# RWKV-7 chain in a hybrid trunk: outputs of four chunks issued together, five state tiles, start tile of the substitution written by memsets

## The chip, the cores and the metric

The kernel runs on one core of one Trainium2 chip. The metric is the device time of one execution in microseconds (us). The engines named below are TensorE (PE in the profile; its weight loads are PEld), VectorE (DVE), ScalarE (ACT), GpSimd (POOL) and SyncE (SP), which here only issues DMAs.

## The reference

One layer of a decoder trunk over 1024 tokens of 1024 features, float32. After an RMS norm one projection feeds three groups of heads; their outputs (256 + 512 + 256 features) are concatenated, projected and added to the residual; a gated MLP with a short convolution and a last norm follow.

```python
h = rms_norm(x, norm_mix)
p_conv, p_nsa, p_rwkv = split(h @ w_in)
mix = concatenate([conv_mixer(p_conv), nsa_mixer(p_nsa), rwkv7_mixer(p_rwkv)])
x = x + mix @ w_out
x = x + conv_ffn(rms_norm(x, norm_ffn), w_gate, conv_w, conv_b, w_up, w_down)
return rms_norm(x, norm_final)
```

The change lies in `rwkv7_mixer`: four heads of 64, each with a 64 x 64 state S that is updated token by token, followed by a norm over each head (group norm), a bonus term and a gate:

```python
def step(S, (r, w, k, v, kk, a)):
    sa = einsum('bhvk,bhk->bhv', S, -kk)
    S = S * w + outer(sa, kk * a) + outer(v, k)
    return S, einsum('bhvk,bhk->bhv', S, r)
```

## The kernel before

The 1024 tokens stay in chunks of 64 for RWKV. Two heads form a pair (j = 0, 1), the tokens form two halves of eight chunks (h = 0, 1), so there are four units, 00, 01, 10 and 11. Each unit passes through three steps. S (`rwkv_prep`, `rwkv_mats`, L487) builds the chunks' matrices; at its end a strictly triangular 32 x 32 system per chunk and head is solved by substitution in 31 pairs of operations on GpSimd (L532, L534), which starts from an identity: L527 copies the constant tile sI (128 x 256) into sT. The rows of the system come back into sN by a DMA from the scratch tensor dn, and sT goes out to dt by DMAs at L537. V (`rwkv_solve`, L542) finishes the inverse for 64 tokens. C (`rwkv_chain`, L583) walks the eight chunks in order.

A chunk in C is a serial loop through two engines: PE multiplies the state H with AT (L595), DVE adds the result into VA (L596), PE forms the state's increment from VA and KB (L601), DVE writes the next state into rH (L608, the two diagonal blocks). Beside this loop the chunk's output is summed in PSUM: r times the old state (L612) plus GR times VA (L615), into its slice of the bank py. There are two rH tiles, used in turn. py is taken from the PSUM tag "rw", which has two banks, before the first chunk; the products of L595 and L601 take turns in what is left of this tag. After the eighth chunk DVE and ACT do the group norm on py (L621 to L632), PE transposes the result (L635) and multiplies the gate (L640), and z (gz) goes to the DRAM tensor md by L642.

The order of the program is the list "lora r0 S00 conv taps V00 S01 keys q C00 V01 r1a cmp0 r1b cmp1 r1c S10 C01 V10 S11 C10 V11 C11", then the attention tiles (`attn_tile`), then the output projection. A tile scheduler simulates the kernel at build time and settles each engine's own order from it; S, V and C are emitted at high priority, so their instructions are put between those of projections (C00) and attention (the other chains).

In an attention tile PE computes scores (L897, L898), transposes the probabilities (L922) and multiplies V (L930); ACT empties the result into a mix tile (L936), and SP stores it to md (L937). The compressed branch has L843, L866, L869. The output projection works by tiles of 128 tokens, the last tile (7) first: two loads of md (`mix`, L988, four 128-feature slabs each: the first holds convolution and RWKV, the second attention), a split of each into two parts (ACT L120, DVE L121), 48 matmuls at L229, and the residual xn (L992). w_out's last pieces (wraw, L971), the norm's gains (grow, L1340) and the first MLP weights (wr and wraw, L1060) are loaded by SP around that place. A wait on any of SP's DMAs holds back what SP has behind it.

Of the kernel before, what the change touches and what calls it, by code (L numbers as in the profile page):

```python
# [7 lines left out]
F32 = mybir.dt.float32  # L8
# [8 lines left out]
P = 128  # L17


class K:  # L20
# [293 lines left out]
    def rwkv_params(self):  # L314
        nc, a = self.nc, self.a
        self.lw_w = self.mc.tile([P, 256], F32, name="lw_w")
        nc.sync.dma_start(self.lw_w[0:32, :], a["rwkv_w2"][0])
        nc.sync.dma_start(self.lw_w[32:64, :], a["rwkv_a2"][0])
        nc.sync.dma_start(self.lw_w[64:128, :], a["rwkv_g2"][0])

        self.bones = self.mc.tile([P, P], F32, name="bones")
        nc.gpsimd.memset(self.bones, 0.0)
        nc.gpsimd.memset(self.bones[0:64, 0:64], 1.0)
        nc.gpsimd.memset(self.bones[64:128, 64:128], 1.0)

        self.rH = [self.mc.tile([P, P], F32, name=f"rH{i}") for i in range(2)]
        for t in self.rH:
            nc.gpsimd.memset(t, 0.0)

        self.sN = self.mc.tile([P, 1024], F32, name="sN")  # L330
        self.sT, self.sI, self.sTT = (self.mc.tile([P, 32, 8], F32, name=n) for n in ("sT", "sI", "sTT"))
        self.sx = self.mc.tile([P, 80], F32, name="sx")
        self.DF = self.mc.tile([P, 16, 32], F32, name="DF")
        nc.gpsimd.memset(self.sI, 0.0)
        for g in range(4):
            r = self.sI[g * 32:g * 32 + 32].rearrange("p a b -> p (a b)")
            nc.gpsimd.memset(r[:, g * 8:256:33], 1.0)

        self.rst = self.mc.tile([P, 512], F32, name="rst")
        nc.gpsimd.memset(self.rst, 1.0)  # L340
        nc.gpsimd.memset(self.rst.rearrange("p (c t) -> p c t", t=64)[:, :, 0:1], 0.0)

        self.gmask = self.mc.tile([P, P], F32, name="gmask")
        nc.gpsimd.memset(self.gmask, 1.0)
        for base in (0, 64):
            for col, strict in ((0, 1), (64, 0)):
                blk = self.gmask[base:base + 64, col:col + 64]
                nc.gpsimd.affine_select(out=blk, in_=blk, pattern=[[1, 64]], compare_op=ALU.is_ge, fill=0.0,
                                        base=-strict, channel_multiplier=-1)
# [135 lines left out]
    def rwkv_mats(self, u):  # L485
        nc = self.nc
        v, s, pe = nc.vector, nc.scalar, nc.tensor  # L487
        dn = self.dram.tile([32, 32, 32], F32, name=f"dn{u.j}{u.h}")
        u.dt = self.dram.tile([16, 32, 4, 8], F32, name=f"dt{u.j}{u.h}")
        u.dtt = self.dram.tile([32, 8, 4, 32], F32, name=f"dtt{u.j}{u.h}")  # L490

        u.GA, u.GR = ([self.rb([P, 8, 64], name=n) for _ in range(2)] for n in ("GA", "GR"))
        for q in range(2):
            pts = [self.bank(u.tp) for _ in range(2)]
            for c in range(4):
                for hp in range(2):
                    r = slice(hp * 64, hp * 64 + 64)
                    pe.matmul(pts[hp][:, c * P:c * P + P], u.BK[q][r, c].rearrange("p a t -> p (a t)"),
                              u.AR[q][r, c].rearrange("p a t -> p (a t)"), start=True, stop=True)
            for x, G in enumerate((u.GA, u.GR)):  # L500
                for hp in range(2):
                    v.tensor_tensor(G[hp][:, q * 4:q * 4 + 4, :], pts[hp].rearrange("p (a b) -> p a b", b=P)[:, :, x * 64:x * 64 + 64],
                                    self.gmask[:, x * 64:x * 64 + 64].unsqueeze(1).to_broadcast([P, 4, 64]), op=ALU.mult)
        for hp in range(2):
            for blk in range(2):
                p0 = blk * 16 + hp * 8
                nc.sync.dma_start(dn[p0:p0 + 8].rearrange("p s t -> s p t"), u.GA[hp][64 + blk * 32:96 + blk * 32, :, blk * 32:blk * 32 + 32])
        N = self.sN.rearrange("p (a b) -> p a b", b=32)
        for g in range(4):
            nc.sync.dma_start(N[g * 32:g * 32 + 32], dn)  # L510
        u.VA, u.KB = [], []
        for q in range(2):
            VA = self.rb([P, 4, P], name="VA")
            KB = self.rb([P, 4, P], name="KB")
            BK = u.BK[q].rearrange("p c a t -> p c (a t)")
            v.tensor_tensor(BK, BK, u.PC[:, q * 4:q * 4 + 4].unsqueeze(2).to_broadcast([P, 4, P]), op=ALU.mult)
            for dst in (VA, KB):
                pt = self.bank(u.tp)
                for c in range(4):
                    x = u.VAc[q][:, c].rearrange("p a t -> p (a t)") if dst is VA else BK[:, c, :]  # L520
                    pe.transpose(pt[:, c * P:c * P + P], x, self.idn)
                s.activation(dst.rearrange("p c x -> p (c x)"), pt, AF.Copy)
            u.VA.append(VA)
            u.KB.append(KB)

        Tm = self.sT
        nc.gpsimd.tensor_copy(Tm, self.sI)  # L527
        for q in range(31):
            n, w = 31 - q, q // 4 + 1
            x = self.sx[:, 0:n * w].rearrange("p (a b) -> p a b", b=w)  # L530
            v_ = getattr(nc, self.B["sub"])
            v_.tensor_tensor(x, N[:, q, q + 1:32].unsqueeze(2).to_broadcast([P, n, w]),  # L532
                            Tm[:, q, 0:w].unsqueeze(1).to_broadcast([P, n, w]), op=ALU.mult)
            v_.tensor_tensor(Tm[:, q + 1:32, 0:w], Tm[:, q + 1:32, 0:w], x, op=ALU.add)  # L534
        sTT = self.sTT.rearrange("p a b -> p (a b)").rearrange("p (a b) -> p a b", b=32)
        v.tensor_copy(sTT, Tm.rearrange("p a b -> p b a"))
        for g in range(4):  # L537
            nc.sync.dma_start(u.dt[:, :, g, :], Tm[g * 32:g * 32 + 16])
            nc.sync.dma_start(u.dtt[:, :, g, :], sTT[g * 32:g * 32 + 32])
# [43 lines left out]
    def rwkv_chain(self, u):  # L583
        nc = self.nc
        v, s, pe = nc.vector, nc.scalar, nc.tensor
# [1 line left out]
        if u.h == 0:  # L587
            self.H = None
        H = self.H
        py = self.bank("rw")  # L590
        for c in range(8):
            VA, KB = u.VA[c // 4][:, c % 4, :], u.KB[c // 4][:, c % 4, :]
            if H is not None:
                pt = self.bank("rw")
                pe.matmul(pt[64:128, 0:P], u.AT[:, c, :], H, start=True, stop=True)  # L595
                v.tensor_tensor(VA[64:128], pt[64:128, 0:P], VA[64:128], op=ALU.add)  # L596
            last = u.h == 1 and c == 7
            if not last:
                pt = self.bank("rw")
                for x in (slice(0, 64), slice(64, 128)):  # L600
                    pe.matmul(pt[x, 0:P], KB[:, x], VA, start=True, stop=True)  # L601
                Hn = self.rH[c % 2]
                for hp in range(2):
                    x = slice(hp * 64, hp * 64 + 64)
                    if H is None:
                        v.tensor_copy(Hn[x, x], pt[x, x])
                    else:
                        v.scalar_tensor_tensor(Hn[x, x], H[x, x], u.PC[x, c:c + 1], pt[x, x], op0=ALU.mult, op1=ALU.add)  # L608
            ro = slice((c % 2) * 64, (c % 2) * 64 + 64)
            yo = (c // 2) * P  # L610
            if H is not None:
                pe.matmul(py[ro, yo:yo + P], u.r[:, c, :], H, start=True, stop=False)  # L612
            for hp in range(2):
                x = slice(hp * 64, hp * 64 + 64)
                pe.matmul(py[ro, yo + hp * 64:yo + hp * 64 + 64], u.GR[hp][:, c, :], VA[:, x], start=H is None, stop=H is None or hp == 1)  # L615
            H = None if last else Hn
        self.H = H

# [787 lines left out]
```

## Time and profile before

| | |
|---|---|
| three runs | 1479.73, 1487.43, 1487.57 us; median 1487.43 us |
| profiled execution | 1479.4 us, of which the span from first to last instruction is 1477.5 us |
| PE busy | 1388.7 us, 94% |
| DVE, ACT, POOL busy | 68%, 46%, 34% |
| mean granted clock of PE | 0.971 |
| chain of work that ended last | PE 79%, DVE 8%, POOL 4%, DMA 3%, ACT 2% |

The span can be read in four stretches: norms and projections with the convolution up to about 344 us, a change of phase with the attention's loads to 377 us, attention to 704 us with three of the four RWKV chains woven in, output projection and MLP to the end. Busy time counts an engine at work; idle time of PE is what a change can win beside fewer or shorter matmuls, and it is read from the rows where a PE instruction shows an idle time ahead of it.

### The profile page before, as it was taken

To read this page: it belongs to the slowest core of one execution; us is meant where nothing else is said; L and a number is where in the kernel's file an instruction comes from. 1 tells how busy PE (TensorE), PEld (TensorE's weight loads), DVE (VectorE), ACT (ScalarE), POOL (GpSimd) and SP (SyncE) were. 2 spreads that over 40 slices of the span, in tenths; PEclk is the share of its full clock that TensorE was granted. 3 is DMA by queue.
4 is the path that set the end of the run, shared out by engine and by line. 5 is a ranking of instruction groups with operands and counts; after the bars stand their busy time and mean duration, and the time that the engine had idled before them with its cause. 6 is when DMAs were issued, how large, how long until landed. Compare 5 with 4: busy or idle time off the path is not lost.

```text
span 1477.5 us, 22767 instructions
## 1 busy us (share of the span) xinstructions
PE 1388.7 (94%) x7897; PEld 1095.2 (74%) x7897; DVE 1002.7 (68%) x2187; ACT 686.9 (46%) x1377; POOL 499.2 (34%) x607
## 2 busy tenths in 40 slices
PE   6999589998899999999799899999999999999997
PEld 5887457776677676766588677888788788888886
DVE  6347594454868778798257867676775776666685
ACT  5441245624456665678223533343343333445463
POOL 1002996921144066220000144443444442113310
PEclk9999888999899999999899999999999999999999
DMA  6133133436514254542722123332332334986533
GB/s 185 40 107 82 44 103 111 142 84 179 153 33 139 78 154 125 181 150 81 240 89 83 43 93 93 108 107 70 104 113 93 108 100 162 388 280 216 188 92 114
DMA packets 206679, 186.69 MB, mean 126 GB/s; under 512 B 56355, under 2 KB 145764, under 8 KB 206564
## 3 DMA queue, kind: packets, MB, share of 16 engines
q1 hardware_dynamic: 206564, 185.24, 40.3%
q8 instruction: 62, 1.02, 0.3%
q14 instruction: 53, 0.43, 0.1%
HBM read 126.99 MB, written 58.20 MB: 125 GB/s over the span
## 4 chain that ended last, share of the span: by engine, by line
PE 79%; DVE 8%; POOL 4%; DMA 3%; ACT 2%; issue 2%; SPq 1%; ACTq 0%; DVEq 0%; POOLq 0%
PE gb L229 13%; PE mm L229 12%; PE rw L229 10%; PE ga L229 9%; PE gc L229 8%; PE tr L229 5%; PE tr L922 5%; PE av L930 4%; PE mm L897 2%; PE mm L898 2%; POOL sT L534 1%; POOL sx L532 1%; DVE pp L901 1%; POOL cacc L279 1%; DVE pp L915 1%
## 5 line engine op out<-in xcount | busy, mean ns | idle before, releaser
L229 PE MATMUL mm<-hT,whi 128*128 128x512 f32 x608 | 200.3, 409 | 19.6 <-DVE ev L690 14.8
L229 PEld LDWEIGHTS mm<-hT,whi 128*128 128x128 f32 x608 | 115.7, 193 | 48.9 <-ACT whi L120 20.2
L229 PE MATMUL mm<-hT,wlo 128*128 128x512 f32 x304 | 123.0, 407 | 1.9 <-DVE wlo L121 1.9
L925 ACT ACTIVATE pT<-tr 128x512 f32<-128x512 f32 (+1 forms) x152 | 79.9, 536 | 60.6 <-PE tr L922 59.2
L930 PE MATMUL av<-pT,V 128*64 128x128 f32 x1056 | 96.0, 287 | 1.5 <-ACT pT L925 1.5
L1076 POOL TENSOR_TENSOR S<-wraw,wr 128x512 f32<-128x512 f32 x22 | 28.5, 1296 | 192.8 <-DVE or L107 91.1
L922 PE MATMUL tr<-idn,pp 128*128 128x128 f32 x528 | 90.3, 289 | 1.8 <-DVE pp L915 1.8
L279 POOL TENSOR_TENSOR cacc<-cacc,ctap 128x512 f32<-128x512 f32 x60 | 85.1, 1429 | 12.7 <-ACT ctap L278 12.4
L121 DVE TENSOR_TENSOR sp<-rb,sp 128x512 fp32r<-128x512 f32 x66 | 55.6, 842 | 49.4 <-ACT sp L120 49.4
L229 PE MATMUL rw<-woh,mix 128*128 128x512 f32 x240 | 79.5, 407 | 9.0 <-ACT mix L120 9.0
L229 PE MATMUL rw<-sp,sp 128*128 128x512 f32 x330 | 86.0, 389 | 0.0
L229 PE MATMUL tr<-sp,sp 128*128 128x512 f32 x330 | 85.9, 389 | 0.0
L897 PE MATMUL mm<-KH,QS 128*128 128x512 f32 (+2 forms) x192 | 77.7, 411 | 3.1 <-DVE mx L901 2.8
L930 PEld LDWEIGHTS av<-pT,V 128*64 128x64 f32 x1056 | 59.2, 136 | 28.3 <-issue 13.7
L922 PEld LDWEIGHTS tr<-idn,pp 128*128 128x128 f32 x528 | 55.9, 141 | 30.5 <-issue 29.1
L915 DVE TENSOR_SCALAR pp<-pp,sm 128x640 f32<-128x640 f32 (+7 forms) x128 | 76.5, 638 | 0.9
L120 ACT ACTIVATE sp<-rb 128x512 fp32r<-128x512 f32 x66 | 41.6, 630 | 74.1 <-PE tr L229 36.5
L121 DVE TENSOR_TENSOR sp<-b,sp 128x512 fp32r<-128x512 f32 x88 | 72.1, 827 | 5.2 <-ACT sp L120 5.0
L229 PEld LDWEIGHTS mm<-hT,wlo 128*128 128x128 f32 x304 | 58.5, 193 | 18.1 <-DVE wlo L121 3.8
L229 PEld LDWEIGHTS tr<-sp,sp 128*128 128x128 f32 x330 | 61.9, 188 | 12.9
L229 PEld LDWEIGHTS rw<-sp,sp 128*128 128x128 f32 x330 | 61.9, 188 | 12.9
L532 POOL TENSOR_TENSOR sx<-sN,sT 128x60 f32<-128x60 f32 (+24 forms) x124 | 48.0, 387 | 63.0 <-DMA sN<-dn 54.9
(455 smaller groups left out, 3648.8 us busy)
## 6 DMA issues: line engine op xcount, KB each, us to landing
wr<-in_ffn_w_gate_dram SPq DMA_DIRECT2D x44, 256.0 KB
wraw<-in_ffn_w_up_dram SPq DMA_DIRECT2D x44, 256.0 KB
pdS<-prod SPq DMA_DIRECT2D x44, 256.0 KB
b<-pdS SPq DMA_DIRECT2D x44, 256.0 KB
rb<-tdT SPq DMA_DIRECT2D x44, 256.0 KB
pdA<-prod SPq DMA_DIRECT2D x33, 256.0 KB
b<-pdA SPq DMA_DIRECT2D x33, 256.0 KB
wraw<-in_w_in_dram SPq DMA_DIRECT2D x30, 256.0 KB
```

The lines of the kernel that those rows point to most:

```text
L120: self.nc.scalar.activation(hi, src, AF.Copy)
L121: getattr(self.nc, eng).tensor_tensor(lo, src, hi.bitcast(F32), op=ALU.subtract)
L229: mm = lambda l, r, **k: self.nc.tensor.matmul(out, l, r, skip_group_check=more, **k)
L279: nc.gpsimd.tensor_tensor(t[:, o:o + 512], t[:, o:o + 512], z, op=ALU.add)
L532: v_.tensor_tensor(x, N[:, q, q + 1:32].unsqueeze(2).to_broadcast([P, n, w]), Tm[:, q, 0:w].unsqueeze(1).to_broadcast([P, n, w]), op=ALU.mult)
L897: pe.matmul(pts[g][:, 0:n], QS[:, r, g, :], KH[g][hf][:, ks], start=True, stop=False)
L898: pe.matmul(pts[g][:, 0:n], QS[:, r, g, :], KL[g][hf][:, ks], start=False, stop=True)
L915: v.tensor_scalar(Ps[g], Ps[g], sm[:, g:g + 1], None, op0=ALU.mult)
L922: pe.transpose(pt[:, o:o + P], Ps[g][:, kt * P:kt * P + P], self.idn)
L925: s.activation(pT[:, 0:n], pt[:, 0:n], AF.Copy)
L930: pe.matmul(av[g * 64:g * 64 + 64, r * P:r * P + P], self.V[kk // 2][:, kk % 2, vo + g * 64:vo + g * 64 + 64], pT[:, o:o + P], start=first ...
L1076: gp.tensor_tensor(t, x, y, op=op)
```

## The change

The chain no longer multiplies a chunk's output when the chunk is done. It keeps the list Hs of old states, and after chunks 3 and 7 it emits the outputs of four chunks together (new lines L618 and L621); py is taken from the two banks only at the first of these. For that five rH tiles exist, used in a ring that runs on over all units (nH). The constant sI goes; the start tile sT is written by a memset over 128 x 256 and four strided memsets of ones, each time. The matmuls are the same in number and shape.

```diff
--- before.py
+++ after.py
@@ -323,18 +323,15 @@
         nc.gpsimd.memset(self.bones[0:64, 0:64], 1.0)
         nc.gpsimd.memset(self.bones[64:128, 64:128], 1.0)
 
-        self.rH = [self.mc.tile([P, P], F32, name=f"rH{i}") for i in range(2)]
+        self.rH = [self.mc.tile([P, P], F32, name=f"rH{i}") for i in range(5)]
+        self.nH = 0
         for t in self.rH:
             nc.gpsimd.memset(t, 0.0)
 
         self.sN = self.mc.tile([P, 1024], F32, name="sN")
-        self.sT, self.sI, self.sTT = (self.mc.tile([P, 32, 8], F32, name=n) for n in ("sT", "sI", "sTT"))
+        self.sT, self.sTT = (self.mc.tile([P, 32, 8], F32, name=n) for n in ("sT", "sTT"))
         self.sx = self.mc.tile([P, 80], F32, name="sx")
         self.DF = self.mc.tile([P, 16, 32], F32, name="DF")
-        nc.gpsimd.memset(self.sI, 0.0)
-        for g in range(4):
-            r = self.sI[g * 32:g * 32 + 32].rearrange("p a b -> p (a b)")
-            nc.gpsimd.memset(r[:, g * 8:256:33], 1.0)
 
         self.rst = self.mc.tile([P, 512], F32, name="rst")
         nc.gpsimd.memset(self.rst, 1.0)
@@ -524,7 +521,9 @@
             u.KB.append(KB)
 
         Tm = self.sT
-        nc.gpsimd.tensor_copy(Tm, self.sI)
+        nc.gpsimd.memset(Tm, 0.0)
+        for g in range(4):
+            nc.gpsimd.memset(Tm[g * 32:g * 32 + 32].rearrange("p a b -> p (a b)")[:, g * 8:256:33], 1.0)
         for q in range(31):
             n, w = 31 - q, q // 4 + 1
             x = self.sx[:, 0:n * w].rearrange("p (a b) -> p a b", b=w)
@@ -587,9 +586,10 @@
         if u.h == 0:
             self.H = None
         H = self.H
-        py = self.bank("rw")
+        py, Hs = None, []
         for c in range(8):
             VA, KB = u.VA[c // 4][:, c % 4, :], u.KB[c // 4][:, c % 4, :]
+            Hs.append(H)
             if H is not None:
                 pt = self.bank("rw")
                 pe.matmul(pt[64:128, 0:P], u.AT[:, c, :], H, start=True, stop=True)
@@ -599,20 +599,27 @@
                 pt = self.bank("rw")
                 for x in (slice(0, 64), slice(64, 128)):
                     pe.matmul(pt[x, 0:P], KB[:, x], VA, start=True, stop=True)
-                Hn = self.rH[c % 2]
+                Hn = self.rH[self.nH % 5]
+                self.nH += 1
                 for hp in range(2):
                     x = slice(hp * 64, hp * 64 + 64)
                     if H is None:
                         v.tensor_copy(Hn[x, x], pt[x, x])
                     else:
                         v.scalar_tensor_tensor(Hn[x, x], H[x, x], u.PC[x, c:c + 1], pt[x, x], op0=ALU.mult, op1=ALU.add)
-            ro = slice((c % 2) * 64, (c % 2) * 64 + 64)
-            yo = (c // 2) * P
-            if H is not None:
-                pe.matmul(py[ro, yo:yo + P], u.r[:, c, :], H, start=True, stop=False)
-            for hp in range(2):
-                x = slice(hp * 64, hp * 64 + 64)
-                pe.matmul(py[ro, yo + hp * 64:yo + hp * 64 + 64], u.GR[hp][:, c, :], VA[:, x], start=H is None, stop=H is None or hp == 1)
+
+            if c % 4 == 3:
+                if py is None:
+                    py = self.bank("rw")
+                for d in range(c - 3, c + 1):
+                    ro = slice((d % 2) * 64, (d % 2) * 64 + 64)
+                    yo = (d // 2) * P
+                    if Hs[d] is not None:
+                        pe.matmul(py[ro, yo:yo + P], u.r[:, d, :], Hs[d], start=True, stop=False)
+                    for hp in range(2):
+                        x = slice(hp * 64, hp * 64 + 64)
+                        pe.matmul(py[ro, yo + hp * 64:yo + hp * 64 + 64], u.GR[hp][:, d, :], u.VA[d // 4][:, d % 4, x], start=Hs[d] is None,
+                                  stop=Hs[d] is None or hp == 1)
             H = None if last else Hn
         self.H = H
```

The tile scheduler settles where the new groups stand. In the first chain, C00 (its first half; VA and KB are a chunk's inputs, GR and rP the output's factors, rH the states), PE had after each chunk's L601 the two output products and went on with a projection:

```order
L601 MATMUL rw_2728<-VA_1215,KB_1216 64x128 x2
L615 MATMUL rw_2717<-VA_1215,GR_1177 64x64
L615 MATMUL rw_2717<-VA_1215,GR_1178 64x64
L229 MATMUL mm_496_2649<-hT_120,whi_2645 128x512
L229 MATMUL mm_496_2649<-hT_128,whi_2645 128x512
L229 MATMUL mm_500_2683<-hT_100,whi_2638 128x512
```

Now, after the fourth chunk's L601, PE has the outputs of four chunks in a row (the first chunk has no state, hence no L618):

```order
L601 MATMUL rw_2749<-VA_1215,KB_1216 64x128 x2
L621 MATMUL rw_2754<-VA_1215,GR_1177 64x64
L621 MATMUL rw_2754<-VA_1215,GR_1178 64x64
L618 MATMUL rw_2754<-rH_738,rP_1154 64x128
L621 MATMUL rw_2754<-VA_1215,GR_1177 64x64
L621 MATMUL rw_2754<-VA_1215,GR_1178 64x64
L618 MATMUL rw_2754<-rH_739,rP_1154 64x128
L621 MATMUL rw_2754<-VA_1215,GR_1177 64x64
L621 MATMUL rw_2754<-VA_1215,GR_1178 64x64
L618 MATMUL rw_2754<-rH_740,rP_1154 64x128
L621 MATMUL rw_2754<-VA_1215,GR_1177 64x64
L621 MATMUL rw_2754<-VA_1215,GR_1178 64x64
```

The output products of chunks 0 to 2 moved behind the third state; in the second half of each chain, chunks 4 to 7, the scheduler puts L618 and L621 beside L595 and L601 as before.

On PE at the end of attention, where the last chain, C11, hands its normed output (gyc) to the transposes, stood before:

```order
L930 MATMUL av_7701<-pT_7763,V_4513 64x128 x4
L922 MATMUL tr_7814<-idn,pp_7799 128x128 x4
L635 MATMUL rw_4413<-idn,gyc_4390 128x128 x4
L640 MATMUL rw_4421<-lora_772,lw_w 128x512
L930 MATMUL av_7701<-pT_7791,V_4513 64x128 x4
```

And now (lines moved by 7, so L642 is the former L635):

```order
L937 MATMUL av_7717<-pT_7871,V_4529 64x128 x4
L929 MATMUL tr_7922<-idn,pp_7907 128x128 x4
L642 MATMUL rw_4429<-idn,gyc_4406 128x128 x4
L647 MATMUL rw_4437<-lora_772,lw_w 128x512
L937 MATMUL av_7717<-pT_7899,V_4529 64x128 x4
L929 MATMUL tr_7950<-idn,pp_7935 128x128 x4
L937 MATMUL av_7717<-pT_7927,V_4529 64x128 x4
L937 MATMUL av_7717<-pT_7955,V_4529 64x128 x4
L229 MATMUL rw_8126<-woh_7966,mix_8112 128x512
```

The transposes moved back: one block of L929 and three of L937 are left behind them before the output projection's first matmul.

SP's queue at the same place, from the load of tile 7's first part of mix on, was before:

```order
L988 DMA mix_8095<-md 128x4x128
L1060 DMA wr_1948_9172<-in_ffn_w_gate_dram 128x4x128
L1060 DMA wraw_9170<-in_ffn_w_up_dram 128x4x128
L1060 DMA wr_1949_9173<-in_ffn_w_gate_dram 128x4x128
L937 DMA md<-mix_7945 128x4x128
L1060 DMA wraw_9171<-in_ffn_w_up_dram 128x4x128
L1060 DMA wr_1981_9329<-in_ffn_w_gate_dram 128x4x128
L988 DMA mix_8101<-md 128x4x128
L1060 DMA wr_1982_9330<-in_ffn_w_gate_dram 128x4x128
L992 DMA xn_8107<-in_x_dram 128x1024
L992 DMA xn_8179<-in_x_dram 128x1024
```

And now (L944 is the former L937, L995 the former L988, L999 the former L992):

```order
L944 DMA md<-mix_7961 128x4x128
L978 DMA wraw_8054<-in_w_out_dram 64x512 x2
L1347 DMA grow_8083<-in_norm_ffn_dram 128x512
L1347 DMA grow_8084<-in_norm_ffn_dram 128x512
L978 DMA wraw_8061<-in_w_out_dram 64x512 x2
L995 DMA mix_8111<-md 128x4x128
L999 DMA xn_8123<-in_x_dram 128x1024
L999 DMA xn_8195<-in_x_dram 128x1024
L999 DMA xn_8330<-in_x_dram 128x1024
L999 DMA xn_8402<-in_x_dram 128x1024
L999 DMA xn_8537<-in_x_dram 128x1024
L995 DMA mix_8117<-md 128x4x128
```

The first load of mix moved behind the last store of attention, behind w_out's last pieces and grow; the MLP's weights (six loads) moved behind all eight xn and stand ahead of tile 6's first mix.

## Rows read from the trace of the kernel before

**Rows 1.** The page's first and fourth part: busy time, and the last chain by engine.
```profile
PE 1388.7 (94%) x7897; PEld 1095.2 (74%) x7897; DVE 1002.7 (68%) x2187; ACT 686.9 (46%) x1377; POOL 499.2 (34%) x607
...
PE 79%; DVE 8%; POOL 4%; DMA 3%; ACT 2%; issue 2%; SPq 1%; ACTq 0%; DVEq 0%; POOLq 0%
```
**Rows 2.** PE's waits, longest first: total us, times, longest us.
```profile
PE mm L229 <- DVE ev L690: 14.8, 1, 14.8
```
**Rows 3.** Stretches: length, busy us (instructions) by engine, clock, DMA share, GB/s.
```profile
255.00:330.00 75.00, 75.00 (x383) 56.98 (x382) 36.55 (x82) 36.26 (x65) 49.74 (x87) 1.00 0.42 121
...
500.00:550.00 50.00, 47.83 (x403) 35.91 (x402) 40.38 (x131) 29.29 (x63) 21.42 (x38) 0.97 0.41 119
...
709.00:726.00 17.00, 11.18 (x45) 8.43 (x44) 5.70 (x9) 4.67 (x10) 2.89 (x2) 0.90 1.01 364
...
730.00:1477.50 747.50, 726.73 (x3212) 592.82 (x3210) 515.77 (x825) 304.14 (x551) 225.41 (x176) 0.99 0.40 131
```
**Rows 4.** GpSimd in order of time, kernel's start: start, duration (us), operation.
```profile
1.70 0.31 POOL L334 MEMSET sI<- 128x256 f32 x1
...
3.45 0.53 POOL L337 MEMSET sI<- 32x8 f32 x4
...
5.18 0.40 POOL L527 COPY sT<-sI 128x256 f32<-128x256 f32 x1
```
**Rows 5.** PE in order of time, its first norm tile.
```profile
10.85 0.48 PE L205 MATMUL pm<-idn,x 128*128 128x128 f32 x1 [5.52 <-DVE x L189]
```
**Rows 6.** The page's group of the substitution's products: busy, mean ns, idle before.
```profile
L532 POOL TENSOR_TENSOR sx<-sN,sT 128x60 f32<-128x60 f32 (+24 forms) x124 | 48.0, 387 | 63.0 <-DMA sN<-dn 54.9
```
**Rows 7.** DVE's waits on the chain's products.
```profile
DVE rH L608 <- PE rw L601: 12.5, 9, 5.1
DVE VA L596 <- PE rw L595: 12.0, 7, 4.3
```
**Rows 8.** PE in order of time: three gaps in attention.
```profile
477.53 0.97 PE L579 MATMUL rw<-W,sN 64*64 64x64 f32 x13 [1.27 <-ACT W L576]
...
511.36 0.41 PE L922 MATMUL tr<-idn,pp 128*128 128x128 f32 x2 [1.28 <-DVE pp L915]
...
577.44 0.80 PE L897 MATMUL mm<-KH,QS 128*128 128x512 f32 x1 [2.29 <-DVE mx L901]
```
**Rows 9.** DVE in order of time: start and end of C11's group norm.
```profile
674.40 0.69 DVE L621 TENSOR_REDUCE gm<-rw 128x8 f32<-128x512 f32 x1
...
691.97 0.69 DVE L632 TENSOR_TENSOR gyc<-gyc,gr 128x512 f32<-128x512 f32 x1
```
**Rows 10.** PE in order of time: attention's end, output projection (tiles 7 and 6).
```profile
701.01 0.66 PE L930 MATMUL av<-pT,V 128*64 128x128 f32 x8
701.60 0.65 PE L922 MATMUL tr<-idn,pp 128*128 128x128 f32 x4
...
703.11 0.66 PE L930 MATMUL av<-pT,V 128*64 128x128 f32 x8 [0.27 <-ACT pT L925]
706.95 0.71 PE L229 MATMUL rw<-woh,mix 128*128 128x512 f32 x1 [3.19 <-ACT mix L120]
...
719.45 0.39 PE L229 MATMUL rw<-wlo,mix 128*128 128x512 f32 x1
719.67 0.39 PE L229 MATMUL rw<-whi,mix 128*128 128x512 f32 x1
725.87 0.79 PE L229 MATMUL rw<-woh,mix 128*128 128x512 f32 x1 [5.81 <-ACT mix L120]
```
**Rows 11.** SP's issues in order of time, around attention's end.
```profile
701.23 0.43 SPq L988 DMA_DIRECT2D mix<-md  x1
...
704.50 0.68 SPq L937 DMA_DIRECT2D md<-mix  x1
...
709.47 5.03 SPq L992 DMA_DIRECT2D xn<-in_x_dram  x8
```
**Rows 12.** The last chain in order of time, tile 6's first mix: start, length, link.
```profile
715.36 9.75 DMA mix<-md
```

## The prediction

> **What bounds the kernel now.** I read the page's first and fourth part, then the waits of PE, the stretches, and the order of time where PE stands idle. PE is busy for 94% of the span and the last chain is PE for 79%, DVE for 8%, DMA for 3% [rows 1]: the kernel is bound by TensorE. The change leaves PE the same matmuls, so it can act only on PE's idle time, 1477.5 - 1388.7 = 88.8 us, and on the clock that is granted after an idle stretch. What idle time lies where the change has nothing to do has to be taken off first. The longest single wait, 14.8 us on DVE's ev, belongs to the convolution [rows 2]. From 730 us to the end PE lacks 747.5 - 726.7 = 20.8 us [rows 3]; there PE's order does not change. What is left for this change are the four chains, the gaps in attention, and the place where attention ends.
>
> **The chains' serial loop.** In C00 (255 to 330 us) PE is busy for 75.00 of 75.00 us at clock 1.00 [rows 3]: the loop's latency is covered by projections. DVE waits for the loop's products, 12.5 us for L601 and 12.0 us for L595 [rows 7], but DVE's wait costs only if PE then waits for DVE, and no chain operation (VA L596, rH L608) is a releaser in PE's list of waits, whose longest row is shown [rows 2]. The deferral takes L612 and L615 out of the place behind L595 and L601, where nothing waited for them, and puts as many in one block. PE's time is the same, the next state's start can come a little earlier, and PE does not notice. I cost this at 0. The five state tiles cost nothing either: with two, a new state waited for reads that PE had finished a chunk earlier. If the cover were gone, in a stretch without other PE work, a deferred block would stand in the way of a chunk; no chain runs in such a stretch.
>
> **Memsets.** The constant sI goes: 0.31 + 0.53 us of GpSimd at the start [rows 4]; three more rH memsets and the first start tile come in, and all GpSimd work there ends near 6 us, while PE's first norm tile starts at 10.85 us and waits for DVE on x [rows 5]. 0. Each later start tile costs 0.31 + 0.53 = 0.84 us where the copy took 0.40 us [rows 4], so +0.44 us, three times. Ahead of the first product L532 GpSimd sits idle for the DMA of sN, 54.9 us in all [rows 6], and the memsets fit in there: 0. With no cover it would be 1.3 us of GpSimd, not of PE.
>
> **Attention.** The three chains in attention move by some microseconds of PE work. PE's largest gaps there are 1.27, 1.28 and 2.29 us [rows 8], two on attention's own softmax (pp, mx), one on the solve's W. None waits for a chain's state or output bank. A move of DVE's chain work may open or close such gaps: together 4.8 us, and the one stretch of 50 us that I list ran at clock 0.97 [rows 3], which is another 1.5 us for a gap. I take 0, between -4.8 - 3.0 = -7.8 (all gone, two stretches back at clock 1.00) and as much the other way, since nothing in the rows prefers a sign.
>
> **C11's group norm (a new wait).** Before, 691.97 + 0.69 - 674.40 = 18.3 us pass from the first reduction to the normed tile [rows 9], all beside attention's matmuls. In the new order PE has little left between the last output product and the transposes of gyc: five blocks of the V product and five of transposes at 701.60 - 701.01 = 0.59 us each [rows 10], 5.9 us, and about 2.3 us of other work, together some 8.2 us. The work needed meanwhile is the four full-width DVE operations of the norm, at 0.69 us by the two shown [rows 9], ACT's square and the small operations on 8 columns, roughly 5 us by themselves, and attention's DVE operations queued among them, about as much again: an estimate of 10 us. So PE waits about 2 us there; behind it stand attention's last products, which all later work waits for. Bounds: 0 (5 us needed) and 10 us (the 18.3 us as they were). I take +2, nearer to the sum of the single operations, since DVE has less of attention left to do by then.
>
> **End of attention to the output projection.** Call E the end of attention's last product, 703.11 + 0.66 = 703.77 us. Before, tile 7 starts at 706.95 = E + 3.2 after a gap of 3.19 us, its 48 matmuls last until about 719.9, 12.9 us, and tile 6 starts at 725.87 = E + 22.1 after a gap of 5.81 us [rows 10]. At the later pace of 719.67 - 719.45 = 0.22 us, 48 would take 10.6 us, so the slow clock behind such a gap costs some 2.4 us. The first mix was issued at 701.23 [rows 11], before E; from issue to PE took 5.7 us. In the new order it stands behind attention's last store (issue at E + 0.73, 0.68 long [rows 11]) and six more issues at 5.03 / 8 = 0.63 us [rows 11]: issued at E + 5.2, PE starts at E + 10.9 and, slow clock included, ends tile 7 at E + 23.8. Its second mix lies behind five xn: 0.25 + 2.6 + 0.25 MB at 364 GB/s [rows 3], 8.6 us, so there by E + 14 and hidden. Tile 6's first mix lies behind all of it, eight xn and six weight loads: about 6.5 MB since E + 5.2, 17.9 us, landing at E + 23.1, on PE near E + 23.8. So the second gap about vanishes, the first grows, and tile 6 starts at E + 23.8 instead of E + 22.1: +1.7. Only one slow start is left instead of two: -2.4. Net -0.7. Bounds: -8.2 (first gap as before, second gone with its slow start) and +7.5 (first gap as worked out, the second one of 5.8 us kept). I take -0.7, for the transfers decide it and their rate is a row. The MLP's weights that are now loaded later have the tiles of the output projection ahead of them, at 10.6 us and more each: 0.
>
> **Sum.** 0 (chains) + 0 (memsets) + 0 (attention) + 2 (tail) - 0.7 (boundary) = +1.3 us on the profiled execution's 1479.4, about 1481. That execution is at the level of the lowest of the three runs, 1479.73; the other two stand at 1487.5, and the median is 1487.43. Which level the changed kernel's runs take is not to be read from one trace, so I put the number between them: 1483 us. What a measurement of this kernel can tell from no change is about 0.5%, 7.4 us.
>
> **Rivals.** *A freed bank pays.* py no longer holds one of the two banks of "rw" during the first half of a chain, so the products of L595, L601 and the solve can run ahead. For it: the solve's gap of 1.27 us [rows 8] uses that tag, and DVE's 24.5 us of waits [rows 7] show a loop that is not at its limit. Against: these are DVE's waits, and PE is full meanwhile. If it holds, attention's gaps go with their clock (-7.8) and half of the boundary's best case (-4.1): 1479.4 - 11.9, about 1468. The Trainium skill, "Perfetto Trace Analysis", section Matmuls, speaks for this rival: it advises that independent matmul groups rotate through different PSUM banks, so that emptying one overlaps the next group. By it the change would gain; C00's 75.00 busy us out of 75.00 show no such overlap missing there.
>
> *The loads at the boundary arrive late.* Tile 7's start slips by 7.7 us, and tile 6's first mix, behind eight xn and six weight loads, lands after E + 23.1; from there every microsecond counts, and with the second gap of 5.8 us kept this is +7.5, with the tail's +2 together 1479.4 + 9.5, about 1489. For it: before, with eight xn ahead, that load took 9.75 us from issue to landing [rows 12]. Against: at 364 GB/s it just arrives in time. The Trainium skill, "DMA: Bandwidth & Descriptors", section Queues, rings and completion order, says that each DMA engine consumes its ring's descriptors in order, so a small load cannot pass the xn ahead of it; by that this rival's wait would be real as soon as bytes decide. The 9.75 us agree.
>
> *The change does not do what it says.* In the second half of each chain the new order still has L618 and L621 chunk by chunk, so only half of the outputs are deferred; then nothing but the boundary is left to act, 1479 to 1481.
>
> **How the numbers follow.** The forecast, no change that counts, has 0.50, and by itself 1476 to 1491 (both levels, tail and boundary within a few us); most of it is same, with 0.08 faster and 0.04 slower through the levels. The freed bank has 0.25, nearly all faster. The late loads have 0.22, of which 0.16 slower. The empty change has 0.03, same. Together faster 0.32, same 0.48, slower 0.20. The range takes in 1468 of the first rival and, for the second at the upper level, part of its way to 1497: 1468 to 1495.
>
> **What would show it.** C00 still without a gap on PE; no wait of PE on rH or VA; a wait of some 2 us at L642 on gyc; the first matmul of the output projection about 11 us after attention's last product instead of 3.2, and tile 6's first matmul with less than 1 us of idle time. Wrong I am if attention's gaps at the softmax vanish, if GpSimd's memsets delay sT's substitution, or if tile 6 starts later than E + 26.

## The result and the profile after

Slower: 1504.2 us median (1496.5 to 1511.2, six runs) against 1486.1 us before, ratio 1.014 with a 95% interval of 1.011 to 1.017. The forecast, 1483 us in 1468 to 1495, is wrong. The profiled execution has a span of 1500.4 us, 22.9 us more than before. The six executions of each kernel lie within 8 and 15 us of each other, while every stretch below is of one profiled execution. Its page and the head of PE's waits (total us, times, longest):

```profile
PE 1391.0 (93%) x7897; PEld 1097.2 (73%) x7897; DVE 1003.6 (67%) x2187; ACT 688.3 (46%) x1377; POOL 499.8 (33%) x621
...
PE 77%; DVE 10%; DMA 4%; POOL 4%; issue 2%; ACT 2%; SPq 1%; ACTq 0%; DVEq 0%
```
```profile
PE rw L229 <- ACT mix L120: 15.7, 2, 11.4
PE mm L229 <- DVE ev L697: 15.1, 2, 14.9
PE mm L904 <- DVE mx L908: 6.8, 6, 1.9
PE av L937 <- ACT pT L932: 6.5, 4, 2.7
...
PE rw L642 <- DVE gyc L639: 3.1, 2, 2.7
```

The work is the same to 2.3 us of busy PE [rows 1]; most of the time went into waits. I cut the span at four instructions of PE that both kernels have: attention's first product (mm<-kcmp,q), the end of its last product of probabilities and V (E), and the first matmuls of tiles 7 and 6 of the output projection.

| us | before | after | change |
|---|---|---|---|
| start to attention | 376.7 | 376.4 | -0.3 |
| attention | 327.0 | 341.7 | +14.7 |
| of it PE idle | 9.6 | 20.0 | +10.4 |
| E to tile 7 | 3.2 | 11.4 | +8.2 |
| E to tile 6 | 22.1 | 29.5 | +7.4 |
| tile 6 to the end | 751.6 | 752.7 | +1.1 |

Nothing happens ahead of attention: C00, where the deferral stands most plainly, is full as before in this execution. Stretches of the changed kernel (length, busy us and instructions of PE, PEld, DVE, ACT, POOL, clock, DMA share, GB/s), to be read beside [rows 3]:

```profile
255.00:330.00 75.00, 75.00 (x385) 56.93 (x384) 33.11 (x75) 36.20 (x65) 50.11 (x91) 1.00 0.43 124
376.41:401.41 25.00, 23.74 (x104) 18.43 (x104) 19.90 (x69) 7.29 (x17) 2.52 (x2) 0.58 0.47 116
450.00:500.00 50.00, 44.40 (x430) 31.20 (x429) 35.26 (x101) 28.20 (x57) 18.18 (x14) 0.93 0.41 132
...
725.00:742.00 17.00, 12.47 (x43) 10.00 (x44) 3.46 (x5) 2.08 (x5) 0.00 (x0) 0.70 1.03 354
```

And two of the kernel before:

```profile
376.73:401.73 25.00, 23.69 (x140) 18.01 (x141) 24.81 (x89) 12.86 (x29) 3.14 (x4) 0.88 0.65 152
450.00:500.00 50.00, 48.53 (x487) 35.16 (x485) 40.27 (x115) 33.66 (x69) 18.49 (x14) 1.00 0.49 154
```

Of attention's +14.7 us, 10.4 are idle time of PE. The other 4.3 are the same 2810 matmuls taking longer: PE's clock stays at its lower level, 1.2 GHz, until 20.9 us into attention here and until 6.1 us before, so the first 25 us have a mean granted clock of 0.58 against 0.88.

From 450 to 500 us PE lacks 5.6 us, before 1.5 us. PE, DVE and GpSimd of the changed kernel there, each in order of time (start, duration, operation, idle time before it):

```profile
473.22 0.50 PE L904 MATMUL mm<-KH,QS 128*128 128x512 f32 x1 [1.91 <-DVE mx L908]
...
479.17 1.07 PE L642 MATMUL rw<-idn,gyc 128*128 128x128 f32 x4 [2.74 <-DVE gyc L639]
```
```profile
451.93 0.69 DVE L628 TENSOR_REDUCE gm<-rw 128x8 f32<-128x512 f32 x1 [1.69 <-PE rw L621]
...
475.13 3.39 DVE L922 TENSOR_SCALAR pp<-pp,sm 128x896 f32<-128x896 f32 x2
478.44 0.68 DVE L639 TENSOR_TENSOR gyc<-gyc,gr 128x512 f32<-128x512 f32 x1
```
```profile
475.15 1.28 POOL L958 TENSOR_TENSOR wraw<-wraw,whi 128x512 f32<-128x512 f32 x1
476.51 1.52 POOL L959 TENSOR_TENSOR whi<-whi,wraw 128x512 f32<-128x512 f32 x1
```

PE stands at C01's transposes because their input is behind two rescalings of the softmax on DVE, which take 1.7 us each while GpSimd subtracts blocks of the MLP's down weights. C01's norm ran from 451.9 to 479.1 us here, over 27 us. Before, it took 14.7 us and ended at 455.3 us, ahead of GpSimd's first subtraction at 459.0 us:

```profile
440.62 0.69 DVE L621 TENSOR_REDUCE gm<-rw 128x8 f32<-128x512 f32 x1
...
454.63 0.69 DVE L632 TENSOR_TENSOR gyc<-gyc,gr 128x512 f32<-128x512 f32 x1
```
```profile
459.03 1.73 POOL L949 TENSOR_TENSOR wraw<-whi,wraw 128x512 f32<-128x512 f32 x1
```

All three chains in attention end later after its start than before. C11's norm in the changed kernel, for [rows 9], and its end of attention on PE and SP, for [rows 10, 11]:

```profile
700.79 0.69 DVE L628 TENSOR_REDUCE gm<-rw 128x8 f32<-128x512 f32 x1
...
710.56 0.69 DVE L639 TENSOR_TENSOR gyc<-gyc,gr 128x512 f32<-128x512 f32 x1
```
```profile
717.48 0.66 PE L937 MATMUL av<-pT,V 128*64 128x128 f32 x8 [2.70 <-ACT pT L932]
729.53 0.80 PE L229 MATMUL rw<-woh,mix 128*128 128x512 f32 x1 [11.39 <-ACT mix L120]
747.68 0.79 PE L229 MATMUL rw<-woh,mix 128*128 128x512 f32 x1 [4.26 <-ACT mix L120]
```
```profile
718.29 0.50 SPq L649 DMA_DIRECT2D md<-gz  x1
...
724.79 0.59 SPq L995 DMA_DIRECT2D mix<-md  x1
...
734.83 6.78 SPq L1067 DMA_DIRECT2D wr<-in_ffn_w_gate_dram  x4
741.71 0.78 SPq L995 DMA_DIRECT2D mix<-md  x1
```

C11's norm began 26.4 us later than before, while E moved by 14.4 us, so it lies 12 us closer to the end of attention. The store of its output (md<-gz) is issued at E + 0.2; before it was issued at E - 6.7:

```profile
697.10 0.34 SPq L642 DMA_DIRECT2D md<-gz  x1
```

The load of tile 7's first mix needs that store, and stands behind more on SP's queue: E + 6.7 instead of E - 2.5.

### The profile page after: what moved, and what is told of

The parts are those of the page before. It is cut to its first block, busy times and chain, and to the rows that moved or that the text cites. A ratio compares the mean times of both kernels' runs of the same rounds, so it can differ in the third digit from the quotient of the medians.

```text
span 1500.4 us, 22757 instructions
## 1 busy us (share of the span) xinstructions
PE 1391.0 (93%) x7897; PEld 1097.2 (73%) x7897; DVE 1003.6 (67%) x2187; ACT 688.3 (46%) x1377; POOL 499.8 (33%) x621
## 4 chain that ended last, share of the span: by engine, by line
PE 77%; DVE 10%; DMA 4%; POOL 4%; issue 2%; ACT 2%; SPq 1%; ACTq 0%; DVEq 0%
PE gb L229 12%; PE mm L229 12%; PE rw L229 10%; PE ga L229 9%; PE gc L229 8%; PE tr L929 4%; PE tr L229 4%; PE av L937 4%; PE mm L904 2%; PE mm L905 2%; DVE pp L922 2%; POOL sT L533 1%; POOL sx L531 1%; DVE pp L908 1%; DMA wraw<-in_w_out_dram 1%
## 5 line engine op out<-in xcount | busy, mean ns | idle before, releaser
L229 PE MATMUL mm<-hT,whi 128*128 128x512 f32 x608 | 196.9, 404 | 21.0 <-DVE ev L697 15.1
L937 PE MATMUL av<-pT,V 128*64 128x128 f32 x1056 | 94.5, 287 | 6.5 <-ACT pT L932 6.5
L929 PE MATMUL tr<-idn,pp 128*128 128x128 f32 x528 | 91.0, 290 | 0.1
L279 POOL TENSOR_TENSOR cacc<-cacc,ctap 128x512 f32<-128x512 f32 x60 | 84.6, 1422 | 10.9 <-ACT ctap L278 10.7
L937 PEld LDWEIGHTS av<-pT,V 128*64 128x64 f32 x1056 | 58.6, 136 | 32.2 <-issue 13.8
L929 PEld LDWEIGHTS tr<-idn,pp 128*128 128x128 f32 x528 | 57.0, 142 | 29.0 <-issue 28.0
```

The costliest lines, as they stand in the source:

```text
L229: mm = lambda l, r, **k: self.nc.tensor.matmul(out, l, r, skip_group_check=more, **k)
L279: nc.gpsimd.tensor_tensor(t[:, o:o + 512], t[:, o:o + 512], z, op=ALU.add)
L929: pe.transpose(pt[:, o:o + P], Ps[g][:, kt * P:kt * P + P], self.idn)
L937: pe.matmul(av[g * 64:g * 64 + 64, r * P:r * P + P], self.V[kk // 2][:, kk % 2, vo + g * 64:vo + g * 64 + 64], pT[:, o:o + P], start=first ...
```

## The experiments

Each ratio compares with the kernel before on the same chip, with a 95% interval. "After" is the changed kernel, E again the end of attention's last product, and the boundary the stretch from E to tile 6's first matmul; idle time is PE's. The expectation quoted under each edit was written before its run.

**Five tiles and memsets alone.**

```diff
-self.rH = [self.mc.tile([P, P], F32, name=f"rH{i}") for i in range(2)]
+self.rH = [self.mc.tile([P, P], F32, name=f"rH{i}") for i in range(5)]
...
-nc.gpsimd.tensor_copy(Tm, self.sI)
+nc.gpsimd.memset(Tm, 0.0)
...
-Hn = self.rH[c % 2]
+Hn = self.rH[self.nH % 5]
```


> Outputs stay per chunk; only the five state tiles and the memsets of the start tile are taken over. Theory A (the deferral in the first chain shifts the order of everything behind it): as before, 1486 us within 4. Theory B (the memsets, or the state ring, cost GpSimd or a wait in each chain): 1490 us or more, and GpSimd's substitution starts later than before.

The edit stands against the kernel before; outputs stay per chunk. 1480.9 us, 0.999 (0.997 to 1.001); the kernel before beside it took 1483.5 us. Theory A holds, 1 us under the range that I gave: attention 325.4 us, the boundary 22.2 us. Memsets and state ring cost nothing that can be seen.

**Deferral in C00 alone.**

```diff
-if c % 4 == 3:
+gs = 4 if (u.j, u.h) == (0, 0) else 1
+if c % gs == gs - 1:
```


> Deferral of four outputs in the first chain C00 alone, the three chains in attention per chunk. Theory A (order): as slow as the changed kernel, 1500 to 1508 us, attention 10 us or more longer than before, C11's transposes near the end of attention. Theory B (each chain pays for its own deferred block): a third or less of the 18 us, under 1492 us, attention as before.

This edit, and all below that do not say otherwise, stand against the changed kernel. 1500.7 us, 1.013 (1.009 to 1.017): nearly all of the loss, from a change to a chain whose last output product lies 48 us ahead of attention. Attention took 340.8 us with 16.5 us idle, the boundary 27.4 us. PE's places of the loss (same columns):

```profile
476.18 0.66 PE L643 MATMUL rw<-idn,gyc 128*128 128x128 f32 x4 [0.76 <-DVE gyc L640]
...
725.96 0.79 PE L229 MATMUL rw<-woh,mix 128*128 128x512 f32 x1 [10.02 <-ACT mix L120]
743.39 0.50 PE L229 MATMUL rw<-woh,mix 128*128 128x512 f32 x1 [3.88 <-ACT mix L120]
```

No chain here defers inside attention, so a deferred block's own cost (theory B) is not the cause. What C00's deferral changes is the order that the build settles on behind it. z is stored at E - 4.5 here, 4.6 us earlier than in after, and tile 7 still comes at E + 10.0: its load is issued at E + 4.5, behind SP's other loads.

**Deferral in C11 alone.**

```diff
+gs = 4 if (u.j, u.h) == (1, 1) else 1
```


> Deferral in the last chain C11 alone. Theory A (order): nothing upstream moves, 1486 us within 5, output projection starts as before. Theory B (the deferred block itself delays the chain's end): C11's norm ends later, the output projection starts several us later after attention's last product, 1490 to 1496 us.

The other lines are as above. 1476.2 us, 0.995 (0.992 to 0.999): faster than both kernels. C11's transposes come at 691 us, the store of z at 695.98, E - 17.0, and the output projection begins inside attention; the second gap, ahead of tile 6, falls from 5.8 to 1.7 us:

```profile
706.55 0.48 PE L229 MATMUL rw<-woh,mix 128*128 128x512 f32 x1
...
721.09 0.47 PE L229 MATMUL rw<-woh,mix 128*128 128x512 f32 x1 [1.72 <-DVE xn L1006]
```

Neither theory holds: A had said "as before", B has the wrong sign. The last chain ends early here, and nothing is left of the first gap.

**After, loads of mix from ScalarE's queue.**

```diff
-nc.sync.dma_start(mf, self.md[...])
+nc.scalar.dma_start(mf, self.md[...])
```


> The changed kernel, with the output projection's loads of mix issued by ScalarE's queue instead of SyncE's, so that they stand behind no xn, w_out or norm-gain load there. If the boundary's 7.4 us are a matter of the queue: tile 7 starts 5 to 6 us after attention's last product instead of 11.4, tile 6 without a gap, 1492 to 1498 us. If the load is late because the last chain's output is late, or because the transfers share the rate: no more than 2 us back, 1502 to 1506 us. Attention stays as in the changed kernel in either case.

1502.3 us, 1.011 (1.007 to 1.014). The boundary gave back 4.4 us (25.1 us); the median shows little of it. Attention took 334.9 us in the profiled execution, with the same order of PE and DVE in it as in after, whose 341.7 us are thus no fixed size. The whole of that execution took 1490.5 us, 12 us under the run's median. The chain of work that ended last says why the boundary did not give back more (start, length, link), and PE's first matmul:

```profile
710.38 3.07 DMA md<-gz
713.45 0.02 issue
713.47 4.57 DMA mix<-md
```
```profile
718.74 0.79 PE L229 MATMUL rw<-woh,mix 128*128 128x512 f32 x1 [8.52 <-ACT mix L120]
```

Freed of SP's order, the load still waits for the late z: store at E + 0.2, 3.1 us to land, 4.6 us for the load, the split, E + 8.5. So in after SP's queue was worth about 3 of the 8.2 us of tile 7. The rest goes with the late chain, but the two delays overlap: in the run with C00 alone z came 4.6 us earlier and tile 7 only 1.4 us.

**One piece of w_out for all, after and before.**

```diff
+if n >= 1:
+    self.wo[k][dh] = self.wo[0][0]
+    continue
```


> The changed kernel, of w_out's sixteen pieces only the first loaded and split, and used in place of all (left out: fifteen loads and splits; the projection's values differ). Theory W (w_out's late pieces, whose tiles come free only when the last chain ends, hold the last chain's z on DVE and SyncE's queue): tile 7 starts 5 us or less after attention's last product instead of 11.4, tile 6 without a gap; 8 to 12 us below the changed kernel, 1490 to 1496 us. Theory Q (the last chain ends late and SyncE's order does the rest): tile 7 still 8 us or more after it, 1500 us or more.

> The kernel before with the same fifteen pieces of w_out left out, as the control of the run before. Both theories: w_out was done in time here, so tile 7 starts about 3 us after attention's last product as it did, and the time is 1476 to 1486 us.

The second edit is the same, made in the kernel before. 1494.1 us, 1.008 (1.005 to 1.010), and 1468.8 us, 0.992 (0.988 to 0.995). After's time lies in the range of theory W, but its control gained as much. By the place of tile 7 theory W falls: with w_out's traffic gone from DVE and SP, tile 7 of after still starts 11.1 us after E:

```profile
710.07 0.46 SPq L649 DMA_DIRECT2D md<-gz  x1
...
713.03 0.38 SPq L998 DMA_DIRECT2D mix<-md  x1
```
```profile
720.00 0.79 PE L229 MATMUL rw<-woh,mix 128*128 128x512 f32 x1 [11.10 <-ACT mix L120]
```

The two kernels stay 25 us apart. The control gained 12 us where I expected 5 at most: before, too, w_out's loads and splits cost, and tile 7 then starts 1.8 us ahead of E.

**Without GpSimd's subtractions beside attention, after and before.**

```diff
-tt(b[0, 0], b[0, 1], b[0, 0], op=ALU.subtract)   (and the three that follow)
```


> The changed kernel without GpSimd's four subtractions for each block of the MLP's down weights, which run beside attention (left out: 44 subtractions; the MLP's values differ). Theory P (beside GpSimd's subtractions DVE's operations take longer, and C01's norm now lies among them, which makes PE's waits at 467 to 479 us): those waits go from 5.6 us to under 2, attention's idle time falls by 5 us or more, 1494 to 1500 us. Theory D (DVE and ScalarE are full of softmax and norm by themselves in the new order): waits and idle time stay within 2 us, 1501 to 1506 us.

> The kernel before without the same subtractions, as the control. Theory P: little to win, since C01's norm lay ahead of them; attention's idle time falls by 3 us or less, 1478 to 1485 us. Theory D: no change, 1480 to 1487 us.

The second edit is the same, made in the kernel before. 1484.8 us, 1.002 (1.000 to 1.004), and 1472.3 us, 0.994 (0.991 to 0.996). Of after's attention 17.9 us go (341.7 to 323.8 us, idle 20.0 to 6.5), of before's 4.9 (327.0 to 322.1, idle 9.6 to 6.5); the difference between the kernels in this stretch shrinks from 14.7 to 1.7 us.

Not all of the 17.9 us can be laid to the subtractions. 5.4 us lie ahead of the first one, where after's clock was low, and behind 556 us the build settles on another order once they are gone. The clean part is from attention's 133rd to its 529th V product (of 1056): there PE, DVE and ScalarE have the same order in after and in the run without, but for one copy on DVE. After and the run without (columns as for the stretches above):

```profile
436.01:556.62 120.61, 111.32 (x1007) 80.36 (x1006) 92.50 (x290) 70.47 (x147) 31.42 (x29) 0.97 0.39 117
438.17:547.10 108.93, 107.17 (x1007) 79.22 (x1007) 79.74 (x291) 70.25 (x147) 8.00 (x21) 1.00 0.36 111
```

The fourth and the last run, with after's order and the subtractions, take 118.9 and 120.5 us for it, the kernel before 114.6 and its control 114.8 (these two differ in order from 537 us on). So the subtractions cost after's order 10 to 12 us here, and the order before nothing. DVE's 896-wide rescalings from 440 to 500 us (line, shape, count, busy us, mean ns, idle), of after and of the run without:

```profile
L922 DVE TENSOR_SCALAR pp<-pp,sm 128x896 f32<-128x896 f32 x8 | 8.4, 1086 | 0.1
```
```profile
L922 DVE TENSOR_SCALAR pp<-pp,sm 128x896 f32<-128x896 f32 x8 | 5.1, 682 | 0.1
```

Theory P holds in its mechanism, and the gain is more than I gave it, in both kernels. It is not C01's norm alone: PE's waits for the softmax between 529 and 539 us and at 624 us go as well, and C01's norm still takes 21.2 us without the subtractions, as against 14.7 us in the old order. The operation itself slows in the kernel before as well (1284 ns against 683 ns without); there PE had other work meanwhile. As whole kernels the two still differ by 12.4 us without the subtractions; in the profiled executions 8.8 us of difference lie at the boundary and 5.0 us ahead of attention. The Trainium skill, "SBUF — State Buffer", section Who interferes with whom, gives the mechanism: GpSimd and DVE share one pair of ports, and an operation that holds it shuts the other engine out until it ends. The lengths here agree; that the ports are the cause is the page's word, since no run here shows ports.

**After, the subtractions one attention tile later.**

```diff
-ds=((), (0, 1, 2), (3, 4), (5, 6, 7), (8, 9), (10,), (), ())
+ds=((), (), (0, 1, 2), (3, 4), (5, 6, 7), (8, 9), (10,), ())
```


> The changed kernel with GpSimd's subtractions for the MLP's down weights started one attention tile later, so that C01's norm is over before they begin. Theory P (DVE slowed beside these subtractions turns into PE's waits): no wait of 1.9 and 2.7 us at C01's transposes, attention 5 to 10 us shorter than in the changed kernel unless another norm meets them; 1492 to 1499 us. Theory D (the order by itself): attention stays 338 us or longer, 1500 us or more.

1502.5 us, 1.012 (1.006 to 1.017). The waits at 467 to 479 us went as theory P said, and the time did not: waits came back beside the subtractions, which now begin at 517.8 us.

```profile
532.65 0.50 PE L904 MATMUL mm<-KH,QS 128*128 128x512 f32 x1 [2.55 <-DVE mx L908]
...
621.26 0.50 PE L904 MATMUL mm<-KH,QS 128*128 128x512 f32 x1 [2.47 <-DVE mx L908]
```

Attention 338.5 us, boundary 30.5 us. As a remedy it fails.

**Deferral in C01 alone.**

```diff
+gs = 4 if (u.j, u.h) == (0, 1) else 1
```


> Deferral in the second chain C01 alone. By theory A (order), C10 and C11 move as far as in the changed kernel and the output projection's loads stand as there, but C01's norm ends some three V products earlier: the boundary is as late as in the changed kernel (tile 6 at 27 us or more after attention's last product), attention in between; 1488 to 1500 us. Theory F (only the first chain's deferral does harm): as before, 1486 us or less.

The other lines are as above. 1489.9 us, 1.004 (1.001 to 1.006). Between, as theory A said: attention 331.3 us, but the boundary 27.9 us, nearly as late as in after. The two losses come apart: most of the boundary's is here, less than a third of attention's. C10 alone was not tried.

**C11 alone, subtractions later.** The edits of the third and of the ninth kernel together.

> Deferral in C11 alone, with GpSimd's subtractions one attention tile later; an attempt at a version that beats both. If the two gains add: attention's gap of 1.3 us before the solve and its neighbours go, 1468 to 1474 us. If the later subtractions only meet other work of DVE: 1474 to 1482 us.

1484.2 us, 1.000 (0.997 to 1.002), above both ranges that I gave. There is no gain to add: the ninth run had none, and here C11's is lost too. The best version stays the one with C11 alone.

**After, the bank held from the start.**

```diff
-py, Hs = None, []
+py, Hs = self.bank("rw"), []
```


> The changed kernel with the output bank py taken before the first chunk, as in the kernel before; every engine has the same order as in the changed kernel. If the free bank mattered at run time, in either direction: 5 us or more from the changed kernel. If not: 1504 us within 5, with the same waits.

1505.4 us, 1.014 (1.008 to 1.020), with after's waits at the same instructions:

```profile
473.92 0.50 PE L904 MATMUL mm<-KH,QS 128*128 128x512 f32 x1 [1.90 <-DVE mx L908]
479.81 0.66 PE L642 MATMUL rw<-idn,gyc 128*128 128x128 f32 x4 [2.68 <-DVE gyc L639]
...
733.74 0.80 PE L229 MATMUL rw<-woh,mix 128*128 128x512 f32 x1 [11.74 <-ACT mix L120]
```

With the same order on every engine, when the bank is taken makes no difference that four runs can tell (theirs lie between 1495.1 and 1514.1 us). The rival of the freed bank is out, in both directions, as far as that.

This execution shows a wait that after's does not, in the middle of C00: one of DVE's splits takes 5.50 us (0.73 us in after), and PE waits for the next one. GpSimd's operations run there without a pause, each as short as it is anywhere nearby; the split ends 0.5 us after the first pause, which is ScalarE's doing.

```profile
276.83 5.50 DVE L121 TENSOR_TENSOR ev<-q,ev 128x512 fp32r<-128x512 f32 x1 [1.69 <-ACT ev L120]
```
```profile
281.46 0.33 POOL L533 TENSOR_TENSOR sT<-sT,sx 128x66 f32<-128x66 f32 x1
283.70 1.72 POOL L279 TENSOR_TENSOR cacc<-cacc,ctap 128x512 f32<-128x512 f32 x1 [1.92 <-ACT ctap L278]
```
```profile
282.99 0.79 PE L229 MATMUL mm<-hT,wlo 128*128 128x512 f32 x1 [3.46 <-DVE wlo L121]
```

The seventh and the ninth run show the same 5.50 us and a wait of 3.5 us. In these three attention begins at 382.7 to 383.9 us, in the four others that defer in C00 at 375.1 to 376.4 us. None of the seven profiled executions without that deferral has it. That is too few to tell whether the deferral brings it about.

## Why the prediction was wrong

**Chains and memsets, 0 each: right for the profiled execution.** There PE has no gap in C00. It waits for no state, the bank makes no difference (last run), and GpSimd's memsets cost nothing that can be seen (first run). But three other executions with C00 deferred begin attention 6 to 9 us later, behind a wait for DVE in the middle of C00. The prediction did not reckon with it, and whether the deferral causes it is open.

**Attention, 0 within 7.8: the step that failed.** I wrote that the chains move "by some microseconds of PE work" and that "nothing in the rows prefers a sign". Measured: +14.7 us in this execution; +7.9 and +12.3 us in two others that keep its order throughout attention (fourth and last run: 334.9 and 339.3 us). C11's norm began 26 us later, and three things that the trace of the kernel before held did prefer a sign. DVE is the busier of the engines that PE waits for; GpSimd's subtractions run on beside attention; and C01's norm was done just ahead of them. Once it lay among them, norm and softmax met on a slowed DVE, and PE's queue had C01's transposes in line behind it. The seventh run puts 10 to 12 us on the subtractions, of which the meeting with C01's norm shows 5.6 us of waits in after; about 5 us of the 14.7 are the longer low stretch of the clock. I had listed three gaps that could close and none that could open.

**C11's tail, +2: the place right, the wait elsewhere.** At the transposes PE waited 0.40 us, not 2, with a norm of 10.5 us, near the 10 estimated; but it waited 1.1, 1.2 and 2.7 us for ScalarE's pT around them. A wait of the kind that I looked for here, of the transposes for gyc, stood at C01: 2.7 us.

**Boundary, -0.7: mis-sized by one assumption.** Tile 7 was put at E + 10.9 and came at E + 11.4. Tile 6 was put at E + 23.8 and came at E + 29.5: I let SP issue at 0.63 us each throughout, while its four loads of wr took 6.8 us to issue and SP waited 2.7 us for landings of xn ahead of MLP loads. So tile 6's first mix was issued at E + 23.6, not E + 15, it landed 5.2 us later, and the second gap, 4.3 us, stayed:

```profile
741.71 5.21 DMA mix<-md
```

That is the second rival, priced at +7.5 and measured at +7.4. I gave it 0.22 and took its condition, a landing later than E + 23.1, for the unlikely case; it landed at E + 28.8. The agreement to 0.1 us is luck: tile 7 started 0.5 us later and lasted 1.0 us longer than priced, and the gap was 1.5 us shorter. Its mechanism was half seen: it laid tile 7's delay to SP's order and tile 6's to bytes on the way. SP's order gave about 3 us of tile 7's delay (fourth run), the rest goes with the late store of z; and tile 6's load was late because it was issued late.

**The cause.** In the profiled execution the deferral costs nothing where it happens. It changes the order that is settled for everything behind it, and in the first chain alone it brings nearly all of the loss (second run). The loss itself arises where the chains then lie: among GpSimd's subtractions in attention, and closer to its end at the boundary. What in the scheduler's reckoning turns a regrouping in C00 into a shift of C01 was not tried and stays open.

**Not settled: the clock.** Into attention, the lower level of PE's clock lasts 20.9 us in after's execution, 6.1 us before, 7.8 us in the run with the mix loads on ScalarE and 5.6 us in the one with the bank held. The last two have after's order in attention, so the long stretch is no fixed part of the change. After needs 59.6 us from attention's start to its 133rd V product, those two 54.6 and 54.0 us: it cost this execution about 5 us. The run with C00 alone has such a stretch too, 18.1 us, and so has the kernel before without w_out, 23.3 us. What makes it long in some executions stays open; the medians of after and of the run with the bank held are alike.

## What to carry to other kernels

When a scheduler settles the order, an edit that is free by itself is priced by what it moves: compare the new order at the places where chains end, and ask which engine is slowed or full there. When two executions differ, hold them against each other stretch by stretch where their order is the same: only there does a difference belong to the edit. A serial side chain that ends with slack to spare is an asset; when it slides towards the end of its cover, what follows it pays. Before deferring in every place, try each alone: here, of the three tried, one was worth 0.5%, and one by itself cost 1.3%.

## What the runs showed of the hardware

DVE's 128x896 rescaling took 682 ns without GpSimd's 128x512 subtractions and 1086 to 1284 ns on average in a stretch with them; a 128x8 operation (L115) among them took 1.23 us at 466.19 us and 0.15 us at 469.97 us. One 128x512 split on DVE took 5.50 us, in three executions alike, while GpSimd ran operations without a pause; in after the same one took 0.73 us. Leaving out the 44 subtractions gained 0.6% before and 1.2% after, the new order behind them included. SP's issue, mostly 0.4 to 0.6 us, took 6.8 us for four loads (2.72, 0.58, 2.51 and 0.83 us) in a stretch with a DMA share of 1.03. Before, eight loads of xn took 5.0 us at a share of 1.01, so a full DMA alone does not account for it.
